# Hybrid mLSTM/HGRN2 layer on one core: value turns split between VectorE and ScalarE, exponential-first gates, a sixth side bank

## The chip, the cores and the metric

The kernel runs on one core of a Trainium2 chip. A core has a matrix engine (TensorE, PE in the profile, with its weight loads as PEld), VectorE (DVE), ScalarE (ACT), GpSimd (POOL) and SyncE (SP), which issues DMAs. Each engine works through its own instruction list in order, and the engines wait for one another by semaphores. SBUF and PSUM have 128 partitions; the kernel uses PSUM as eight banks.

The metric is the device time of one execution in microseconds. Before the change it is 2304.08 us, the median of 3 runs (2303.45 to 2305.43).

## The reference

One layer of a decoder on 320 tokens (256 of a prompt, 8 x 8 of a sample) with D_MODEL 2048, all in float32. Two token mixers, an mLSTM (4 heads, key 256, value 512) and an HGRN2 (8 heads, key 128, value 256), read one input projection. They are recurrences that carry a state over the tokens and that the reference evaluates in chunks of 64. Cut to what matters here:

```python
proj = jnp.einsum('btd,de->bte', x, w_in)
(ml_q, ml_k, ml_v, ml_i, ml_f, ml_o, hg_q, hg_f, hg_i, hg_g, gate_a, gate_b) = jnp.split(proj, offs, axis=-1)
...
h, C, n, m = _mlstm(q, k, v, ig, lf, C0, n0, m0)
branch_a = layernorm(h) * ml_norm_g * jax.nn.sigmoid(ml_o)
f = lbh + (1.0 - lbh) * jax.nn.sigmoid(_heads(hg_f, HG_HEADS))
o, S = _hgrn2(hq, jnp.log(f), 1.0 - f, _heads(hg_i, HG_HEADS), S0)
branch_b = o * rsqrt(mean(o * o) + eps) * hg_norm_g * jax.nn.silu(hg_g)
ya = branch_a @ w_branch_a
yb = branch_b @ w_branch_b
merged = jax.nn.sigmoid(gate_a) * ya + jax.nn.sigmoid(gate_b) * yb
x1 = LayerNorm(ALPHA * x + merged @ w_out)
y = LayerNorm(ALPHA * x1 + jnp.square(jax.nn.relu(x1 @ w_up)) @ w_down)
# out: y, and the new states C, n, m, S
```

## The kernel before

**Main work.** All activations lie channel by token: 128 channels on the partitions, 320 tokens in the columns. The weights are cut into 304 tiles of 128 output channels by 2048 input channels. Each tile is summed into one PSUM bank by 48 matmuls of 128x320, 16 input blocks by 3 products: weights and activations are each split into a high and a low fp32r part (`wh`/`wl`, `xh`/`xl`), and the products are high-high, high-low and low-high. A tile comes in two units of 128x1024 weights. For each unit SP loads `wr`, ACT makes `wh` from it (a copy, in line 350, the helper that records every ACT operation), and DVE makes `wl = wr - wh` (line 497). Three such `wh`/`wl` buffers go round; ACT may write one when PE has finished the unit that used it.

**Order.** The main matmuls have a fixed order: 4 mLSTM heads (tiles mv, mk, mq), with gate tiles ga between them, 8 HGRN heads (two gate tiles, then hf, hq and two hi each), 16 output-gate tiles o, the rest of the gates, then hg, wa, wb, wo, and the two feed-forward products. All else is written as chains (Python generators) which a planner, `Sched`, puts between the main matmuls while the program is built. The planner keeps a clock per engine and prices each operation by functions: `act(n)` is (112 + n)/1.2 ns, `dve(n)` (66 + n)/0.96, `dve_t(n)` for DVE transposes. A side matmul is placed in PE's list when the planner's clock says that its operand is ready, with 450 ns to spare (`PE_LAT`). Nothing is reordered at run time: if an operand comes later than planned, PE waits with all that stands behind.

**Banks.** Three PSUM banks (`mbank`) take the main tiles and five (`sbank`) the side matmuls, from the start until tile hg 0 and on until wo 0, where they are dealt out anew.

**Values.** The values of a head come from the main tiles as channel by token and are needed as token by channel. `turn` does this by DVE transposes, which turn blocks of 32x32, in 24 pieces a head: each piece reads one group of 32 partitions and writes another. For an mLSTM head (`m_V`) they are 16 of 32x256 and 8 of 32x128, for an HGRN head (`h_i`) 16 of 32x128 and 8 of 32x64. In `h_i` the last pieces are followed by a high part on ACT (`rh<-f`, 64x256), a low part on DVE (line 1488 before, 1492 after), and two side matmuls `rh,ra` of 128x256, which spread the sample's values over the partitions (lines 1492 and 1493 of before, with `self.spread`).

**Gates.** `sigmoid` takes a gate's main bank. DVE writes min(-p, 87) to SBUF (line 1309), ACT takes the exponential, ACT the logarithm of 1 plus it, scaled, ACT the exponential of minus that, which gives the reciprocal, and DVE does a correction step in two operations (lines 1315 and 1316). 72 tiles pass through it. `free` names the bank that is released as soon as the first operation has read it.

**Outputs.** `h_out` normalises an HGRN head's prompt output (`rms`, with a copy, a Square and one-column operations) and transposes two blocks of 128x256 (line 1631). `ev_o` multiplies an output gate with the mLSTM output and splits the product into high and low parts (line 1672) for the products wa.

Of the kernel before, what the change touches and what calls it, by code (L numbers as in the profile page):

```python
# [12 lines left out]
AF = mybir.ActivationFunctionType  # L13
ALU = mybir.AluOpType
# [6 lines left out]
TOK = 320  # L21
KT = 16
MH, DK, DV = 4, 256, 512
HH, HK, HV = 8, 128, 256
EPS = 1e-5
LN_SH = 62
# [218 lines left out]
def wait(*evs):  # L245
    return ("wait", evs)


def acq(pool, n=1):
    return ("acq", pool, n)  # L250


def rel(pool, item):
    return ("rel", pool, item)


def post(ev):
    return ("set", ev)


def act(n, psum=False, ptr=0):
    return ((61 if psum else 112) + n) / 1.2 + 93 * ptr


def dve(n, psum=False, mode=1, ptr=0):
    return ((62 if psum else 66) + n / mode) / 0.96 + 55 * ptr


def dve_t(n):
    return 155.0 + 1.07 * n  # L270


def pe_f(n, m=128):
# [40 lines left out]
class Program:  # L314
# [48 lines left out]
    def carve(self):  # L363
# [12 lines left out]
        self.Part = Part  # L376
        A, B, C, R = Part(self.f1), Part(self.f2), Part(self.f3), Part(self.ra[:, 0:6400])

# [5 lines left out]
        self.vr = Pool([A.three(4, 320)])  # L384
        self.kw = Pool([B.three(2, 320)])
        self.bc = Pool([B(712) for _ in range(2)])
        self.eb0 = B(512)
        self.eb = Pool([self.eb0])
        self.stg = Pool([B(256) for _ in range(2)])
        self.qn0 = B(256)  # L390
        self.qn = Pool([self.qn0])
# [190 lines left out]
    def before(self, i, t):  # L582
        s = self.s
        kind, h, c = t[:3]
        if kind == "mv" and c == 0:
            s.until(lambda: self.vr.free and self.qk.free)
            self.m_start(h)
            self.vr.free.sort(key=lambda x: x[0])
            self.mh[h]["vr"] = self.vr.free.pop(0)[1]
        elif kind == "hf":  # L590
            s.until(lambda: self.hs.free)
            if h == 0:
                s.spawn(self.m_after(), 0)
            self.h_start(h)
        elif kind == "o" and h == 0:
            s.until(lambda: all(m["end"].t is not None for m in self.mh))
        elif kind == "hg" and h == 0:
            s.until(lambda: all(m["end"].t is not None for m in self.hh))
            self.carve_m()
            self.carve_b()  # L600
            B = self.Part(self.f2)
            for pool in (self.sg, self.sg, self.sr, self.ld, self.ld, self.ld):
                pool.free.append((s.t["pe"], B(320)))
        if kind in ("o", "wa", "hg", "wb"):
            s.spawn(self.fetch(kind, h), 1)
        elif kind == "mk" and h == 0 and c == 0:
            self.load_ev.t = s.t["pe"]
            self.dma(self.lmask, self.d["lmask"])
        elif kind == "wo" and h == 0:
            s.until(lambda: len(self.sbank.free) >= 5)  # L610
            self.mbank.free += self.sbank.free[:3]
            del self.sbank.free[:3]
            self.hl_free += [(s.t["pe"], x) for x in self.wx[:4]]
            R = self.Part(self.wxv[4].rearrange("p x s v -> p (x s v)"))
            self.lns = [R.three(2, TOK) for _ in range(3)]
            s.spawn(self.ln_x(), 1)
        elif kind == "dn" and c == 3 and h == 0:
            self.carve_x()
        elif kind == "dn" and c == 0 and h == 0:
            s.spawn(self.xs_(), 0)  # L620
        elif i == len(TILES) - 8:
            for j in range(MH):
                s.spawn(self.m_C(j), 3)
            for j in range(HH):
                s.spawn(self.h_S(j), 3)
# [519 lines left out]
    def turn(self, to, x):  # L1145

        v = self.nc.vector
        n = x.shape[1]
        for a in range(4):
            p = slice(32 * a, 32 * a + 32)  # L1150
            col = lambda y: y.rearrange("p (c a k) -> p a c k", a=4, k=32)[:, a]
            for b in range(4):
                q = slice(32 * b, 32 * b + 32)
                i = x[p, :, 0:NP_].rearrange("p c (i b k) -> p b i c k", b=4, k=32)[:, b]
                o = to[q, 0:2, :].rearrange("p i (c a k) -> p a i c k", a=4, k=32)[:, a]
                yield ("dve", dve_t(64 * n), lambda: v.transpose(o, i))  # L1156
            for b in range(2):
                o, i = col(to[64 + 32 * b:96 + 32 * b, 2, :]), x[p, :, NP_ + 32 * b:NP_ + 32 * b + 32]
                yield ("dve", dve_t(32 * n), lambda: v.transpose(o, i))  # L1159

    def later(self):
        e = Ev()
# [140 lines left out]
    def sigmoid(self, p, out, r, free=()):  # L1303

        v = self.nc.vector
        yield ("dve", dve(TOK, True), lambda: v.tensor_scalar(out, p, -1.0, 87.0, ALU.mult, ALU.min))  # L1309
        for pool, x in free:  # L1310
            yield rel(pool, x)
        yield ("act", act(TOK), lambda: self.A(out, out, AF.Exp))
        yield ("act", act(TOK), lambda: self.A(r, out, AF.Ln, scale=2.0 ** -LN_SH, bias=self.ln_b))
        yield ("act", act(TOK), lambda: self.A(r, r, AF.Exp, scale=-1.0, bias=self.exp_b))
        yield ("dve", dve(TOK), lambda: v.scalar_tensor_tensor(out, out, 1.0, r, ALU.add, ALU.mult))  # L1315
        yield ("dve", dve(TOK), lambda: v.scalar_tensor_tensor(out, out, 2.0, r, ALU.subtract, ALU.mult))  # L1316

    def ev_hf(self, h, c, b):
# [296 lines left out]
    def h_out(self, h):  # L1615
        nc, v, m = self.nc, self.nc.vector, self.hh[h]
        if h:
            yield wait(self.hh[h - 1]["o"])
        yield wait(m["aT"], m["I"])
        at, it = m["at"], m["it"]  # L1620
        on = yield acq(self.on)
        yield post(m["o"])
        b = yield acq(self.sbank)
        yield ("pe", pe_f(256), lambda: self.mm(b[:, 0:256], at[:, 0:128], it[:, 0, :], start=True, stop=True))
        yield ("pe", pe_f(256), lambda: self.mm(b[:, 256:512], at[:, 368:496], it[:, 0, :], start=True, stop=False))
        yield ("pe", pe_f(256), lambda: self.mm(b[:, 256:512], at[:, 128:256], it[:, 1, :], start=False, stop=True))
        for i in range(2):
            yield from self.rms(b[:, 256 * i:256 * i + 256], on[:, i, :], 128)
        yield rel(self.sbank, b)
        for i in range(2):  # L1630
            yield ("dve", dve_t(256), lambda: v.transpose(on[:, i, :], on[:, i, :]))  # L1631
        yield from self.place(self.rows_to(self.oH[h]), on[:, 0:2, :].rearrange("p i v -> p (i v)").rearrange("p (b c) -> p b c", c=32))
        done = self.later()
        yield wait(m["S"])
        ob = m["ob2"]
        yield from self.rms(ob[:, 0:256], on[:, 2, :], 128)
        yield rel(self.sbank, ob)
        yield rel(self.at, at)
        b = yield acq(self.sbank)
        for j in range(2):  # L1640
            yield ("pe", PE_T, lambda: nc.tensor.transpose(b[:, 128 * j:128 * j + 128], on[:, 2, 128 * j:128 * j + 128], self.ident))
        o = yield acq(self.ho)
        for j in range(2):
            yield ("act", act(64, True), lambda: self.A(by_row(o, 64 * j, False), by_row(b, 128 * j, True)))
        yield rel(self.sbank, b)
        yield ("sp", 620, lambda: self.dma(
            self.oL[h].rearrange("(j p) t -> p j t", p=128), o[:, 0:128].rearrange("p (j t) -> p j t", t=64)))
        for j in range(2):
            yield post(self.oT_ev[2 * h + j])
        yield wait(self.later())  # L1650
        yield rel(self.ho, o)
        yield wait(done)
        yield rel(self.on, on)
        yield wait(m["SP"], m["sdone"])
        yield rel(self.it, it)
        yield rel(self.hs, m["set"])
        yield post(m["end"])
# [33 lines left out]
    def ev_o(self, j, c, b):  # L1691
        v = self.nc.vector
        g = yield acq(self.sg)
        r = yield acq(self.sr)
        yield from self.sigmoid(b[:, :TOK], g, r, ((self.mbank, b),))
        yield rel(self.sr, r)
        x = yield from self.fetched("o", j)
        yield ("dve", dve(TOK, ptr=1), lambda: v.scalar_tensor_tensor(g, g, self.vec[:, V_MLG + j:V_MLG + j + 1], x, ALU.mult, ALU.mult))  # L1698
        yield rel(self.ld, x)
        yield from self.split(g, self.bah[:, j, :], self.bal[:, j, :])  # L1700
        yield rel(self.sg, g)
        yield post(self.ba_ev[j])
# [386 lines left out]
```

## Time and profile before

| what | value |
| --- | --- |
| median of 3 runs | 2304.08 us |
| profiled execution, whole | 2302.73 us |
| its span in the profile | 2300.8 us |
| PE busy | 2289.6 us, 15592 matmuls |
| DVE busy | 1458.9 us, 2634 instructions |
| ACT busy | 1036.6 us, 1653 instructions |
| POOL busy | 13.5 us |
| PE's granted clock | full speed in all 40 slices |
| DMA | 424.94 MB, a mean of 185 GB/s |

The profile is of one execution; PE, PEld, DVE, ACT and POOL are engines, and `L350` is line 350 of the kernel. A row of the groups reads: line, engine, operation, out <- in with partitions x elements, count, busy us and mean ns of one, and then the idle time of the engine just before these instructions and what ended it. Names of tiles are those of the memory that they lie in: `f`, `f3h` are float32 scratch, `ra`, `rh` fp32r scratch, `misc` single columns, `bank` a PSUM bank. The matmuls are pipelined, so a matmul's own length (0.31 us) is longer than the time from one to the next (0.146 us). A row of waits reads: engine and what waited, what it waited for, total us, times, longest us.

### The profile page before, as it was taken

The numbers are of one execution on the slowest core, as the hardware profiler recorded it, in microseconds if no ns is written. First come the engines' busy times: TensorE is split into PE (matmuls) and PEld (weight loads), VectorE is DVE, ScalarE is ACT, GpSimd is POOL, SyncE is SP. The second block draws the span as 40 slices with busy tenths as digits, with TensorE's granted clock in tenths as the row PEclk, the third lists the DMA queues.
The fourth block names the chain that finished last, engine by engine and source line by source line (L and its number), as shares of the span: only waits on it lengthen the run. The fifth ranks groups of instructions, "written<-read, shape, count | busy, mean of one in ns | idle before, by whom it ended". The sixth has DMA issues, their size and how long they took to land.

```text
span 2300.8 us, 38921 instructions
## 1 busy us (share of the span) xinstructions
PE 2289.6 (100%) x15592; PEld 2246.1 (98%) x15592; DVE 1458.9 (63%) x2634; ACT 1036.6 (45%) x1653; POOL 13.5 (1%) x37
## 2 busy tenths in 40 slices
PE   9999999999999999999999999999999999999998
PEld 9999899999999999999999999999999999999998
DVE  6786786788888886555555767654444444444455
ACT  5443445455555565444433446533433343234334
POOL 0000000000000000000000000000000000000000
PEclk9999999999999999999999999999999999999999
DMA  7667977755565564555545644444444444444475
GB/s 284 211 186 259 295 250 229 259 176 185 191 207 187 166 198 167 180 174 170 176 172 175 214 163 147 147 147 149 154 147 150 152 147 153 149 147 154 149 228 193
DMA packets 214574, 424.94 MB, mean 185 GB/s; under 512 B 83572, under 2 KB 110068, under 8 KB 213368
## 3 DMA queue, kind: packets, MB, share of 16 engines
q1 hardware_dynamic: 209512, 415.97, 53.7%
q0 software_dynamic: 4736, 6.29, 1.0%
q8 instruction: 122, 2.00, 0.3%
q14 instruction: 60, 0.49, 0.1%
q10 hardware_dynamic: 144, 0.20, 0.0%
HBM read 371.48 MB, written 50.90 MB: 184 GB/s over the span
## 4 chain that ended last, share of the span: by engine, by line
PE 69%; DVE 3%; ACT 1%; issue 0%; ACTq 0%; DVEq 0%
PE bank L356 69%; DVE wl L497 1%; ACT wh L350 0%; DVE f L1156 0%; DVE f L1445 0%; ACT f L350 0%; DVE f3m L1973 0%; DVE f3m L1980 0%; ACT f3m L350 0%; DVE f L1159 0%; DVE f L1315 0%; DVE f L1316 0%; DVE f L1631 0%; DVE f L1698 0%; DVE f L1309 0%
## 5 line engine op out<-in xcount | busy, mean ns | idle before, releaser
L356 PE MATMUL bank<-xh,wh 128*128 128x320 f32 (+1 forms) x2504 | 794.6, 318 | 0.0
L356 PE MATMUL bank<-xh,wl 128*128 128x320 f32 (+1 forms) x2504 | 774.8, 310 | 0.0
L356 PE MATMUL bank<-xl,wh 128*128 128x320 f32 (+1 forms) x2504 | 772.2, 309 | 0.0
L497 DVE TENSOR_TENSOR wl<-wr,wh 128x1024 fp32r<-128x1024 f32 x440 | 538.7, 1224 | 361.4 <-ACT wh L350 358.3
L350 ACT ACTIVATE wh<-wr 128x1024 fp32r<-128x1024 f32 x440 | 465.4, 1058 | 524.7 <-PE bank L356 495.6
L356 PEld LDWEIGHTS bank<-xh,wh 128*128 128x128 f32 x2504 | 472.0, 189 | 17.2 <-issue 15.3
L356 PEld LDWEIGHTS bank<-xl,wh 128*128 128x128 f32 x2504 | 471.5, 188 | 3.3
L356 PEld LDWEIGHTS bank<-xh,wl 128*128 128x128 f32 x2504 | 471.8, 189 | 0.2 <-DVE wl L497 0.2
L497 DVE TENSOR_TENSOR bb<-wr,bb 128x1024 fp32r<-128x1024 f32 x162 | 198.5, 1225 | 193.7 <-ACT bb L350 193.5
L350 ACT ACTIVATE bb<-wr 128x1024 fp32r<-128x1024 f32 x162 | 171.6, 1059 | 294.6 <-PE bank L356 277.5
L356 PE MATMUL bank<-ra,wh 128*128 128x320 f32 x1008 | 275.9, 309 | 0.7 <-DVE ra L1672 0.7
L356 PE MATMUL bank<-ra,bb 128*128 128x320 f32 x1096 | 255.2, 309 | 0.0
L356 PE MATMUL bank<-xh,bb 128*128 128x320 f32 (+1 forms) x1136 | 253.8, 309 | 0.0
L356 PE MATMUL bank<-rxb,bb 128*128 128x320 f32 x1088 | 249.0, 309 | 0.0
L356 PEld LDWEIGHTS bank<-xh,bb 128*128 128x128 f32 x1136 | 191.0, 188 | 0.0
L356 PE MATMUL bank<-rxb,wh 128*128 128x320 f32 x608 | 187.5, 308 | 0.0
L356 PE MATMUL bank<-rxb,wl 128*128 128x320 f32 x608 | 187.5, 308 | 0.0
L356 PEld LDWEIGHTS bank<-ra,bb 128*128 128x128 f32 x1096 | 184.9, 187 | 0.0
L356 PEld LDWEIGHTS bank<-rxb,bb 128*128 128x128 f32 x1088 | 184.2, 187 | 0.0
L356 PEld LDWEIGHTS bank<-ra,wh 128*128 128x128 f32 x1008 | 180.9, 187 | 0.9 <-DVE ra L1672 0.9
L356 PE MATMUL bank<-xl,bb 128*128 128x320 f32 (+1 forms) x568 | 175.5, 309 | 0.0
L356 PE MATMUL bank<-bb,wh 128*128 128x320 f32 (+1 forms) x536 | 119.0, 313 | 0.0
(259 smaller groups left out, 2244.4 us busy)
## 6 DMA issues: line engine op xcount, KB each, us to landing
wr<-wt SPq DMA_DIRECT2D x602, 512.0 KB, 3.3
rx<-C SPq DMA_DIRECT2D x34, 256.0 KB, 5.6
Cs<-rx SPq DMA_DIRECT2D x34, 256.0 KB, 4.8
f<-C SPq DMA_DIRECT2D x30, 256.0 KB, 5.5
Cs<-f SPq DMA_DIRECT2D x30, 256.0 KB, 4.1
f<-first SPq DMA_DIRECT2D x6, 704.0 KB, 9.6
vD<-ra SPq DMA_DIRECT2D x4, 1024.0 KB, 5.2
f<-S SPq DMA_DIRECT2D x8, 512.0 KB, 5.0
```

Of the source, the lines that this page charges most:

```text
L350: return self.nc.scalar.activation(out, in_, func, **kw)
L356: self.nc.tensor.matmul(*a, **kw)
L497: self.V().tensor_tensor(lo, raw, hi.bitcast(F32), ALU.subtract)
```

## The change

Six edits are made together.

1. `turn`: one DVE transpose turns the whole value tile in place (128x1280 in an mLSTM head, 128x640 in an HGRN head). The 24 pieces become ACT copies of the same shapes, from one group of 32 partitions to another; each waits for the transpose.
2. `sigmoid`: ACT takes exp(-p) from the bank at once, and the bank is released after it. DVE then clamps the result to 1e38 and adds 1, ACT takes the scaled logarithm and the exponential, and DVE's correction is a plain product and one more operation.
3. A sixth side bank: from the first mk tile until hg 0, one main bank is lent to the side matmuls, so that the main tiles have two.
4. `h_out`: one transpose of 128x512 in place of two of 128x256.
5. `ev_o`: from the eighth output gate on, the split waits for an event of the last HGRN head (`aT`, or `sdone` from the thirteenth).
6. The planner's price `dve_t` of a DVE transpose.

```diff
@@ dve_t
-    return 155.0 + 1.07 * n
+    return 295.0 + 1.05 * n
@@ before()
             self.carve_b()
+            self.mbank.free.append(self.sbank.free.pop())
...
         elif kind == "mk" and h == 0 and c == 0:
+            s.until(lambda: self.mbank.free)
+            self.sbank.free.append(self.mbank.free.pop())
@@ turn()
         n = x.shape[1]
+        t = yield ("dve", dve_t(TOK * n), lambda: v.transpose(x, x))
         for a in range(4):
...
-                yield ("dve", dve_t(64 * n), lambda: v.transpose(o, i))
+                yield ("act", act(64 * n), lambda: self.A(o, i), (t,))
...
-                yield ("dve", dve_t(32 * n), lambda: v.transpose(o, i))
+                yield ("act", act(32 * n), lambda: self.A(o, i), (t,))
@@ sigmoid()
-        yield ("dve", dve(TOK, True), lambda: v.tensor_scalar(out, p, -1.0, 87.0, ALU.mult, ALU.min))
+        yield ("act", act(TOK, True), lambda: self.A(out, p, AF.Exp, scale=-1.0))
         for pool, x in free:
             yield rel(pool, x)
-        yield ("act", act(TOK), lambda: self.A(out, out, AF.Exp))
-        yield ("act", act(TOK), lambda: self.A(r, out, AF.Ln, scale=2.0 ** -LN_SH, bias=self.ln_b))
-        yield ("act", act(TOK), lambda: self.A(r, r, AF.Exp, scale=-1.0, bias=self.exp_b))
-        yield ("dve", dve(TOK), lambda: v.scalar_tensor_tensor(out, out, 1.0, r, ALU.add, ALU.mult))
+        yield ("dve", dve(TOK, mode=2), lambda: v.tensor_scalar(out, out, 1e38, 1.0, ALU.min, ALU.add))
+        yield ("act", act(TOK), lambda: self.A(r, out, AF.Ln, scale=2.0 ** -LN_SH))
+        yield ("act", act(TOK, False, 1), lambda: self.A(r, r, AF.Exp, scale=-1.0, bias=self.exp_b))
+        yield ("dve", dve(TOK), lambda: v.tensor_tensor(out, out, r, ALU.mult))
         yield ("dve", dve(TOK), lambda: v.scalar_tensor_tensor(out, out, 2.0, r, ALU.subtract, ALU.mult))
@@ h_out()
-        for i in range(2):
-            yield ("dve", dve_t(256), lambda: v.transpose(on[:, i, :], on[:, i, :]))
+        yield ("dve", dve_t(512), lambda: v.transpose(on[:, 0:2, :], on[:, 0:2, :]))
@@ ev_o()
+        if j > 6:
+            yield wait(self.hh[HH - 1]["aT" if j < 12 else "sdone"])
         yield from self.split(g, self.bah[:, j, :], self.bal[:, j, :])
```

Since the planner sets the order from its prices, the change also moves instructions. Three places in the values of the fifth HGRN head show it. In the rows a shape like 32x4x32 is a piece of 128 columns in four strips, and 32x2x32 one of 64.

On ACT, before, the high part `rh` of these values (third row) stands among copies for other work:

```order
L350 ACTIVATE wh<-wr 128x1024
L350 ACTIVATE ra<-bank_86 32x256
L350 ACTIVATE rh<-f_76 64x256
L350 ACTIVATE ra<-bank_86 32x256
L350 ACTIVATE f_76<-bank_85,misc 128x256
```

On ACT, after, the pieces stand ahead of it, between the rms of the head before, a gate's Exp (from `bank_82`) and Ln, and the weights `wh`; these are the last rows of the burst:

```order
L350 ACTIVATE f_76<-bank_82 128x320
L350 ACTIVATE f_76,misc<-bank_81 128x256
L350 ACTIVATE wh<-wr 128x1024
L350 ACTIVATE f_76<-f_75 32x4x32 x2
L350 ACTIVATE f_76<-f_75 32x2x32 x2
L350 ACTIVATE f_76<-f_75 32x4x32 x4
L350 ACTIVATE f_76<-f_75 32x2x32 x2
L350 ACTIVATE f_76<-f_76 128x320
L350 ACTIVATE misc<-misc 128x1
L350 ACTIVATE rh<-f_76 64x256
L350 ACTIVATE wh<-wr 128x1024
```

The 24 pieces have come into ACT's list, with one `wh` right ahead of them and another among them.

On DVE, before, the last piece (line 1159) and, seven rows behind it, the low part of the same values (line 1488):

```order
L987 TENSOR_TENSOR f_76<-f_75,f_76 128x16x8
L497 TENSOR_TENSOR wl<-wr,wh 128x1024
L1059 TENSOR_TENSOR misc<-misc 128x1
L1416 TENSOR_TENSOR f_75<-f_75 128x16x8
L1159 STREAM_TRANSPOSE f_76<-f_75 32x2x32
L1471 COPY_PREDICATED f_75<-lmask,bank_88 128x16x8
L1060 TENSOR_TENSOR misc<-misc 128x1
L1418 TENSOR_TENSOR f_75<-f_75 128x16x8
L1061 TENSOR_SCALAR misc<-misc 128x1
L1062 TENSOR_TENSOR misc<-misc 128x1
L1419 TENSOR_TENSOR f_75<-f_75 128x16
L1488 TENSOR_TENSOR rh<-f_76,rh 64x256
```

On DVE, after, from the last but one weight part to the low part (line 1492):

```order
L1384 TENSOR_TENSOR ra<-f_75,ra 128x800
L497 TENSOR_TENSOR wl<-wr,wh 128x1024
L1316 TENSOR_SCALAR f_76<-f_76 128x320
L1667 TENSOR_SCALAR misc<-misc 128x1
L1059 TENSOR_SCALAR misc<-misc 128x1
L497 TENSOR_TENSOR wl<-wr,wh 128x1024
L1319 TENSOR_TENSOR f_76<-f_76 128x320
L1062 TENSOR_TENSOR misc<-misc 128x1
L1492 TENSOR_TENSOR rh<-f_76,rh 64x256
```

The pieces are gone from DVE's list, and a `wl`, which waits for the `wh` behind ACT's `rh`, stands three rows ahead of the low part.

On PE, before, the first spread matmul of these values follows 147 main matmuls later in the program than it does after the change:

```order
L356 MATMUL bank_82<-xh,wl 128x320
L1641 MATMUL bank_84<-cst,f_76 128x128
L356 MATMUL bank_88<-rh,ra 128x256
L356 MATMUL bank_82<-xh,wh 128x320
L356 MATMUL bank_82<-xl,wh 128x320
```

On PE, after, it stands three main matmuls into the tile hf of the next head:

```order
L356 MATMUL bank_86<-f_75 128x32
L356 MATMUL bank_82<-xh,wh 128x320
L356 MATMUL bank_82<-xl,wh 128x320
L356 MATMUL bank_82<-xh,wl 128x320
L356 MATMUL bank_84<-rh,ra 128x256
```

The spread has moved up, from the last tile of the next head to its first.

## The prediction

> **What bounds the kernel now.** I read the page's totals first, then PE's waits, then its busy share in stretches, then the groups of the lines that change.
>
> ```profile
> span 2300.8 us, 38921 instructions
> PE 2289.6 (100%) x15592; PEld 2246.1 (98%) x15592; DVE 1458.9 (63%) x2634; ACT 1036.6 (45%) x1653; POOL 13.5 (1%) x37
> PE bank L1530 <- DVE f L987: 1.5, 3, 0.7
> PE bank L356 <- DVE rh L1488: 1.1, 2, 0.6
> PE bank L356 <- POOL ones L640: 1.0, 1, 1.0
> PE bank L1212 <- DVE f L1049: 0.7, 1, 0.7
> PE bank L356 <- DVE ra L1672: 0.7, 1, 0.7
> PE bank L356 <- DMA rx<-C: 0.2, 1, 0.2
> ```
>
> PE is busy all the time. The six rows below the totals are all that it waits for: 5.2 us together (columns: total, times, longest). No edit can win more than that while PE's instructions stay the same, and the change neither adds nor drops one on PE. Four of the six rows (1.5 + 1.1 + 0.7 + 0.2 = 3.5 us) are waits for DVE or a DMA inside the heads, where DVE is relieved; POOL's is the start, L1672's the output gates.
>
> ```profile
> 500.00:600.00 100.00, 99.95 (x703) 97.28 (x702) 86.16 (x240) 56.01 (x123) 0.73 (x2) 1.00 0.62 197
> 700.00:800.00 100.00, 98.78 (x701) 95.22 (x700) 83.82 (x230) 57.19 (x129) 0.37 (x1) 1.00 0.56 180
> 1000.00:1100.00 100.00, 100.00 (x683) 100.00 (x682) 58.54 (x80) 44.01 (x57) 0.00 (x0) 1.00 0.51 171
> ```
>
> These are stretches of 100 us (busy time and count of PE, PEld, DVE, ACT, POOL, then PE's clock). At 1000 us there are only main matmuls: 100.00/683 = 0.1464 us each, and a tile of 48 lasts 7.03 us. At 500 to 800 us, among the HGRN heads, DVE is 84 to 86% busy and ACT 56%. So the change takes work from the fuller engine. But PE runs in order: what decides is whether a side matmul's operand is there when PE gets to it.
>
> **The turn.** The rows of the 288 small transposes, of two wide ones, and of the ACT copies nearest to the new pieces:
>
> ```profile
> L1156 DVE STREAM_TRANSPOSE f<-f 32x128 f32<-32x128 f32 x96 | 29.0, 303 | 2.3
> L1156 DVE STREAM_TRANSPOSE f<-f 32x256 f32<-32x256 f32 x64 | 27.9, 436 | 1.5
> L1159 DVE STREAM_TRANSPOSE f<-f 32x64 f32<-32x64 f32 x48 | 11.4, 238 | 1.0
> L1159 DVE STREAM_TRANSPOSE f<-f 32x128 f32<-32x128 f32 x32 | 9.7, 304 | 0.8
> L1156 DVE STREAM_TRANSPOSE f<-f3h 32x128 f32<-32x128 f32 x32 | 9.7, 302 | 0.7
> L1159 DVE STREAM_TRANSPOSE f<-f3h 32x64 f32<-32x64 f32 x16 | 3.8, 238 | 0.4
> L1631 DVE STREAM_TRANSPOSE f<-f 128x256 f32<-128x256 f32 x16 | 7.0, 435 | 0.0
> L1090 DVE STREAM_TRANSPOSE f<-f 128x512 f32<-128x512 f32 x8 | 5.7, 709 | 0.2
> L350 ACT ACTIVATE rh<-f 64x256 fp32r<-64x256 f32 x8 | 3.3, 415 | 2.1 <-DVE f L1159 1.9
> L350 ACT ACTIVATE ra<-f 64x128 fp32r<-64x128 f32 x4 | 1.2, 308 | 0.1
> L350 ACT ACTIVATE f<-f 64x64 f32<-64x64 f32 x4 | 1.0, 253 | 0.9 <-DVE f L907 0.8
> ```
>
> DVE loses the first six rows, 91.5 us. It gains four transposes of 128x1280 and eight of 128x640. The two wide rows give (709 - 435)/256 = 1.07 ns a column, so 0.85 us for 640 and 1.53 us for 1280: 12.9 us in all. The two 256-wide transposes of the head's output become one of 512: 2 x 0.435 - 0.709 = 0.16 us less for each of 8 heads. DVE nets about -80 us.
>
> ACT gains the 288 copies. By the last three rows a copy of 256, 128 and 64 columns takes 0.415, 0.308 and 0.253 us. Whether two of them overlap is shown by these stretches (start, length, xcount):
>
> ```profile
> 605.69 0.76 ACT L350 ACTIVATE ra<-bank 32x256 fp32r<-32x256 f32 x2 [1.60 <-PE bank L1530]
> 610.49 0.34 ACT L350 ACTIVATE f<-bank 128x64 f32<-128x64 f32 x2
> 614.70 0.77 ACT L350 ACTIVATE f<-bank 32x32 f32<-32x32 f32 x4
> L350 ACT ACTIVATE ra<-bank 32x256 fp32r<-32x256 f32 x32 | 12.0, 374 | 5.5 <-PE bank L1530 5.1
> L350 ACT ACTIVATE f<-bank 128x64 f32<-128x64 f32 x32 | 5.5, 215 | 2.0 <-PE bank L1641 1.0 <-PE bank L1212 0.9
> L350 ACT ACTIVATE f<-bank 32x32 f32<-32x32 f32 x32 | 6.0, 186 | 1.8 <-PE bank L356 1.4
> ```
>
> Two copies over all 128 partitions take 0.34 us, not 2 x 0.215 = 0.43: about 0.09 overlaps. Copies on 32 partitions don't: two of 0.374 take 0.76 and four of 0.186 take 0.77, some 0.01 apart. Every new piece is on 32 partitions, so I take 0.32 us (128) and 0.265 (64): an HGRN head's burst is 16 x 0.32 + 8 x 0.265 = 7.2 us. An mLSTM head's is 16 x 0.427 + 8 x 0.32 = 9.4 us. With overlap by 0.095 it would be 16 x 0.213 + 8 x 0.158 = 4.7 us; these are the two ends. The planner's own price, (112 + n)/1.2, is 0.20 and 0.147, a burst of 4.4 us. So ACT falls some 2.8 us behind the plan in each HGRN head. Before, the planner charged 0.292 and 0.223 for the pieces on DVE, which took 0.303 and 0.238: that plan was nearly right.
>
> The Trainium skill (ScalarE: Activation LUTs, What ACT_TABLE_LOAD costs) gives an ACTIVATE with immediates 186 ns + 0.833 ns per element and lets back-to-back ones overlap by about 93 ns. That would be 0.2 and 0.146 us a piece. The pair on 128 partitions agrees; the 32-partition runs don't, and the measurement decides for these pieces.
>
> **What the lateness hits.** These rows carry the chain:
>
> ```profile
> L350 ACT ACTIVATE wh<-wr 128x1024 fp32r<-128x1024 f32 x440 | 465.4, 1058 | 524.7 <-PE bank L356 495.6 <-issue 21.2 <-DMA wr<-wt 7.1
> L497 DVE TENSOR_TENSOR wl<-wr,wh 128x1024 fp32r<-128x1024 f32 x440 | 538.7, 1224 | 361.4 <-ACT wh L350 358.3 <-PE bank L356 1.2
> L1488 DVE TENSOR_TENSOR rh<-f,rh 64x256 fp32r<-64x256 f32 x8 | 3.4, 421 | 0.8 <-ACT rh L350 0.7
> 612.13 0.36 PE L356 MATMUL bank<-rh,ra 128*128 128x256 f32 x1 [0.63 <-DVE rh L1488]
> L350 ACT ACTIVATE f<-bank 128x320 f32<-128x320 f32 x57 | 24.7, 437 | 95.3 <-PE bank L356 95.2
> L350 ACT ACTIVATE f<-f 128x320 f32<-128x320 f32 x138 | 63.0, 457 | 17.4 <-DVE f L1309 14.8 <-DVE f L1852 2.4
> L350 ACT ACTIVATE f<-bank,misc 128x256 f32<-128x256 f32 x24 | 11.3, 470 | 22.6 <-DVE misc L1062 22.5
> L350 ACT ACTIVATE f<-f,misc 128x320 f32<-128x320 f32 x162 | 91.1, 563 | 32.4 <-DVE f L1937 21.3 <-DVE f L1323 7.0
> ```
>
> After the burst come ACT `rh<-f` 64x256, DVE `rh` (L1488 before, L1492 after), and PE's first `rh,ra` matmul, for which PE already waited 0.63 us at 612. Worked for the fifth head, from the moment when PE finishes the weight unit whose buffer ACT needs. On ACT: `wh` 1.06, the burst 7.2, the rms copy 0.47, a gate's Exp 0.44, a Square of the rms copy's size, 0.47 at most, a second `wh` 1.06, the gate's Ln 0.46, a one-column op (at most a 64-column copy's 0.25), `rh` 0.42; less some 0.1 for each overlap of 128-partition neighbours: 11.3 to 11.6. DVE has a `wl` ahead of L1492, which waits for the next `wh` (12.6) and ends at 13.8; then L1319 and L1062, about 0.5 by L1488's 0.42 for 256 columns, and L1492 0.42: ready at 14.7. PE meets its matmul after 76 main matmuls and seven side ones, counted as a main one each: 83 x 0.1464 = 12.15. The stall is 2.5 us. The same sum for the other heads, with their own orders, gives 0.2 for the first (its place is further off) and 2.0, 2.1, 2.2, 2.3, 2.3, 2.4: together 16.0 us. In the mLSTM heads the pieces' readers and the next weights lie one to three us beyond the burst's end: 0 to 0.3 each, counted as 0.
>
> **The other edits.** They are priced from the last four rows above and from these:
>
> ```profile
> L1309 DVE TENSOR_SCALAR f<-bank 128x320 f32<-128x320 f32 x70 | 34.2, 488 | 40.3 <-PE bank L356 39.7
> L1315 DVE SCALAR_TENSOR_TENSOR f<-f 128x320 f32<-128x320 f32 x70 | 34.3, 490 | 13.5 <-ACT f L350 13.0
> L1316 DVE SCALAR_TENSOR_TENSOR f<-f 128x320 f32<-128x320 f32 x70 | 34.3, 490 | 1.5
> L1323 DVE TENSOR_SCALAR f<-f,misc 128x320 f32<-128x320 f32 x6 | 2.6, 435 | 0.1
> ```
>
> A gate keeps three ops on each engine. ACT: 0.457 + 2 x 0.563 becomes 0.437 + 0.457 + 0.563, 0.126 less; 72 gates, -9 us. DVE: the clamp moves from PSUM (0.488) to SBUF, 0.435 at most by L1323, half of that if immediates run faster: -4 to -18 us. All of it lies beside PE. The main bank is now freed by ACT, perhaps behind part of a burst. Moving one bank leaves main two: a bank is wanted again one tile, 7.03 us, after its last matmul. In the fifth head the Exp follows 14 pieces and runs some 3 us after its tile's end, leaving about 4 us. Cost 0; if that cover went, the next tile would start late by the rest. The sixth side bank removes no row of PE's waits: those name data. The two new waits of an output gate stand on events whose matmuls PE has passed by then: 0; behind them waits only that gate's own split.
>
> **Sum.** 2302.73 us is the profiled execution (span 2300.8 and 1.93 outside it). -3.5 for DVE's waits (0 to -3.5), +16.0 for eight stalls (0 to 20): 2315.2. The median of the runs lies 1.35 above that execution: 2316.6; I say 2316.
>
> **Rivals.** 0.2% is 4.6 us, about what a measurement of this kernel can tell from no change: 2299.5 to 2308.7.
> - The pieces overlap like the 128-partition ops. For it: the pair of 0.34. Against: both 32-partition rows. Each burst is then 2.5 us shorter, all stalls but a few tenths go, and only the 3.5 remain: 2304.08 - 3.5 = 2300.6, not slower. At a mean of about 0.23 us a piece (a 5.5 us burst) stalls of 8 x 0.6 and the gain cancel; below that the change wins. The Trainium skill's rule quoted above (ScalarE: Activation LUTs) leads to this time.
> - Stalls come, but at a third to a half of the size: the `wh` whose buffer I took as late may start sooner, or PE's side matmuls cost more than I counted. 16 becomes 5 to 8: 2304.08 - 3.5 + 5 to 8, 2305.6 to 2308.6, no change.
> - A second wait follows in each head: ACT, 2.8 us late, delivers `wh` late for the next main unit, or a gate's bank is freed late, for 1 us or more beyond the first stall: +8 to +12 more, 2324 to 2328. Against it: ACT is idle 44% of these stretches and three weight buffers stand ahead.
>
> **Chances.** Forecast (2308.7 to 2322) 0.65; a third to a half 0.16; overlap 0.10; second waits 0.09. Overlap ends faster by over 0.2% only if it also clears nearly all 5.2 us: 0.04, with 0.02 for gains that I don't see. So faster 0.06, same 0.20, slower 0.74. The range runs from 2302 (most of the overlap case below it) to 2323.
>
> **What would show it.** Right: the `f<-f` 32x128 copies on ACT at 0.30 to 0.33 us and back to back without overlap; PE's waits headed by DVE `rh` L1492, about eight times 2 us; DVE some 90 us less busy, ACT 85 more. Wrong: 24 pieces within 5 us, no wait for L1492, or waits of the main matmuls for `wh` or for a bank at the top of the list.

## The result, and the profile after

The changed kernel takes 2332.59 us (median of 4 runs, 2329.23 to 2334.51) against 2304.67 us before on the same chip: a ratio of 1.012, 95% interval 1.0103 to 1.0138. It is slower by 28 us; the forecast was slower by 12. Its profiled execution took 2331.51 us, with a span of 2329.4 us.

The totals of the page of the changed kernel, and then all that PE waited for:

```profile
span 2329.4 us, 38935 instructions
PE 2298.8 (99%) x15592; PEld 2255.8 (97%) x15592; DVE 1351.8 (58%) x2350; ACT 1110.0 (48%) x1941; POOL 13.6 (1%) x37
```
```profile
PE bank L356 <- DVE rh L1492: 18.6, 8, 2.6
PE bank L356 <- DVE rx L1275: 2.9, 3, 1.6
PE bank L356 <- DVE ra L967: 1.2, 1, 1.2
PE bank L356 <- POOL ones L643: 1.0, 1, 1.0
PE bank L356 <- DVE ra L1675: 0.7, 1, 0.7
PE bank L356 <- DVE f L1201: 0.3, 1, 0.3
PE bank L1534 <- DVE f L990: 0.2, 1, 0.2
```

DVE is relieved by 107 us and ACT carries 73 more (the forecast had 90 and 85), and the time got worse: neither engine was the bound. The new head of the list is the wait that the forecast named, for the low part of the HGRN values at L1492, eight times, 18.6 us. Below it are 4.4 us of waits in the mLSTM heads (L1275, L967, L1201), which are new. The low part is the operation that was L1488 before, where it cost 1.1 us. Of the other waits of before, those for L1049 and for the DMA are gone, and for L987 (now L990) 0.2 us are left.

One stall in full, that of the fifth head, the one worked out in the prediction. The timelines of ACT, DVE and PE in the changed kernel (start, length, operation):

```profile
644.49 1.05 ACT L350 ACTIVATE wh<-wr 128x1024 fp32r<-128x1024 f32 x1
645.56 3.45 ACT L350 ACTIVATE f<-f 32x128 f32<-32x128 f32 x11
649.13 0.41 ACT L350 ACTIVATE rh<-f 64x256 fp32r<-64x256 f32 x1
649.57 1.06 ACT L350 ACTIVATE wh<-wr 128x1024 fp32r<-128x1024 f32 x1
```
```profile
650.65 1.23 DVE L497 TENSOR_TENSOR wl<-wr,wh 128x1024 fp32r<-128x1024 f32 x1 [3.37 <-ACT wh L350]
651.80 0.49 DVE L1319 TENSOR_TENSOR f<-f 128x320 f32<-128x320 f32 x1
652.20 0.15 DVE L1062 TENSOR_TENSOR misc<-misc 128x1 f32<-128x1 f32 x1
652.38 0.42 DVE L1492 TENSOR_TENSOR rh<-f,rh 64x256 fp32r<-64x256 f32 x1
```
```profile
650.18 0.31 PE L356 MATMUL bank<-xh,wl 128*128 128x320 f32 x1
652.95 0.55 PE L356 MATMUL bank<-rh,ra 128*128 128x256 f32 x1 [2.46 <-DVE rh L1492]
653.30 0.47 PE L356 MATMUL bank<-xh,wh 128*128 128x320 f32 x1
653.57 0.47 PE L356 MATMUL bank<-xl,wh 128*128 128x320 f32 x1
```

The second ACT row merges the last ten pieces and the Ln that stands among them: eleven operations in 3.45 us, a mean of 0.31 us, with no overlap. `rh` ends at 649.54, but DVE has a `wl` first, which waits for the `wh` of 649.57; so L1492 starts at 652.38. PE stands from 650.5 to 652.95. The last two PE rows show the part that was not forecast: the next main matmuls start 0.27 us apart instead of 0.147. PE's clock has fallen. The stretches around this stall, and then around that of the seventh head (columns: stretch, length, PE busy, matmuls, granted clock, share and rate of the DMA):

```profile
648.83:652.24 3.41, 1.66 (x12) 1.00 0.22 85
652.24:655.65 3.41, 2.70 (x10) 0.50 0.71 225
655.65:659.07 3.42, 3.42 (x14) 0.50 0.95 253
659.07:662.48 3.41, 3.41 (x24) 1.00 0.74 228
```
```profile
761.47:764.88 3.41, 1.70 (x12) 1.00 0.52 187
764.88:768.29 3.41, 3.41 (x26) 1.00 1.02 357
```

The granted clock is one half for 6.83 us, and in the second half of that PE, though busy all the time, does 14 matmuls where it would do some 23. That costs about as much as the stall itself: some 2.7 us, by the distances of 0.27 and 0.147 us from the stall's end on. But not every stall has one: the seventh head's is 2.52 us long and the clock stays full. In the whole trace, up to the last matmul, the clock is one half in five places, here for 6.83 us and in the others for 3.41: behind four of the eight stalls (the fourth, fifth, sixth and eighth head) and behind one in the mLSTM heads.

The 28.6 us of span add up like this: PE's listed waits 24.9 - 5.2 = 19.7 us; the time between starts of neighbouring matmuls of 128x320 or 128x322 over the full array, summed over the trace, 2128.0 us against 2119.1, and with five pairs fewer: 9.6 us of lower clock. Together 29.3.

The groups whose durations the forecast had to estimate:

```profile
L350 ACT ACTIVATE f<-bank 128x320 f32<-128x320 f32 x127 | 55.1, 435 | 171.6 <-PE bank L356 171.2
L350 ACT ACTIVATE f<-f 32x128 f32<-32x128 f32 x128 | 39.3, 307 | 4.1 <-DVE f L1152 2.3
L350 ACT ACTIVATE f<-f 32x256 f32<-32x256 f32 x64 | 26.5, 415 | 2.2 <-DVE misc L1062 1.0 <-DVE f L1152 0.5
L350 ACT ACTIVATE f<-f 32x64 f32<-32x64 f32 x48 | 12.2, 253 | 0.6
L1152 DVE STREAM_TRANSPOSE f<-f 128x1280 f32<-128x1280 f32 x4 | 6.0, 1494 | 0.0
L1152 DVE STREAM_TRANSPOSE f<-f 128x640 f32<-128x640 f32 x6 | 5.0, 836 | 0.0
L1316 DVE TENSOR_SCALAR f<-f 128x320 f32<-128x320 f32 x70 | 22.5, 321 | 0.0
```

### The profile page after: what moved, and what is told of

It reads as the page before. It is cut to its first block, busy times and chain, and to the rows that moved or that the text cites. A ratio compares the mean times of both kernels' runs of the same rounds, so it can differ in the third digit from the quotient of the medians.

```text
span 2329.4 us, 38935 instructions
## 1 busy us (share of the span) xinstructions
PE 2298.8 (99%) x15592; PEld 2255.8 (97%) x15592; DVE 1351.8 (58%) x2350; ACT 1110.0 (48%) x1941; POOL 13.6 (1%) x37
## 4 chain that ended last, share of the span: by engine, by line
PE 90%; ACT 6%; DVE 3%; DMA 1%; issue 1%; SPq 0%; ACTq 0%; POOL 0%; DVEq 0%; POOLq 0%
PE bank L356 89%; ACT f L350 4%; ACT wh L350 1%; DVE wl L497 1%; DMA rx<-C 0%; DMA wr<-wt 0%; DMA Cs<-rx 0%; DVE f L1152 0%; DVE f3m L1978 0%; DVE f3m L1985 0%; DVE rx L1275 0%; DVE rh L1492 0%; ACT f3m L350 0%; DVE f L1319 0%; DVE ra L967 0%
## 5 line engine op out<-in xcount | busy, mean ns | idle before, releaser
L350 ACT ACTIVATE f<-f 32x128 f32<-32x128 f32 (+7 forms) x413 | 153.4, 372 | 90.3 <-DVE f L1316 72.7
```

The source lines that it names most:

```text
L350: return self.nc.scalar.activation(out, in_, func, **kw)
```

## The experiments

The theory after the result: the pieces on 32 partitions take 0.12 us more than the planner's price, so PE's list calls for operands before they are there; the longer of the stalls also lower PE's clock for some microseconds. Rivals: the copies are too much for ACT wherever they stand (rival 1); or gates, banks or another edit cost the time, not the turn (rival 2). All times below are medians beside runs of the kernel before on the same chip (2303.7 to 2304.0 us).

**The price alone.** In the changed kernel:

```diff
-                yield ("act", act(64 * n), lambda: self.A(o, i), (t,))
+                yield ("act", act(64 * n) + 118.0, lambda: self.A(o, i), (t,))
...
-                yield ("act", act(32 * n), lambda: self.A(o, i), (t,))
+                yield ("act", act(32 * n) + 118.0, lambda: self.A(o, i), (t,))
```

> The changed kernel, the planner's price of each ACT piece raised by 118 ns (to what the pieces took there: 0.307 us and 0.012 to the next, against 0.200 planned). Theory (pieces on 32 partitions don't overlap, the plan is 2.8 us too early in each HGRN head, PE stalls, and its clock falls after the longer stalls): PE's wait for the low part at L1492 falls from 18.6 to under 3 us, the granted clock rises from 0.995 to 0.999, time 2300 to 2306 us. Rival 1 (the copies are too much work for ACT wherever they stand: they push the weights back): waits go over to others, above 8 us in all beyond the 5.2 of the kernel before, 2315 us or more. Rival 2 (gates or banks cost the time, not the turn): 2325 us or more.

Measured: 2297.29 us, ratio 0.9976 (0.9964 to 0.9988). Every instruction of the change is still there; only the plan differs, and 35 us are gone. The profile page's totals and all of PE's waits in this kernel:

```profile
PE 2286.5 (100%) x15592; PEld 2245.1 (98%) x15592; DVE 1348.5 (59%) x2350; ACT 1110.8 (48%) x1941; POOL 13.4 (1%) x37
```
```profile
PE bank L1030 <- DVE f L990: 1.1, 1, 1.1
PE bank L356 <- POOL ones L643: 1.0, 1, 1.0
PE bank L356 <- DVE ra L1675: 0.7, 1, 0.7
PE bank L1644 <- ACT f L350: 0.2, 1, 0.2
```

ACT is as busy as in the changed kernel (1110.8 against 1110.0 us), and nothing waits for L1492, nor for L1275 or L967 in the mLSTM heads. Rival 1 falls: the work fits. The time is 2.7 us below the expected range, and the run is faster than the kernel before.

**The turn back on DVE,** the rest of the change kept:

```diff
-        t = yield ("dve", dve_t(TOK * n), lambda: v.transpose(x, x))
...
-                yield ("act", act(64 * n), lambda: self.A(o, i), (t,))
+                yield ("dve", 155.0 + 1.07 * 64 * n, lambda: v.transpose(o, i))
...
-                yield ("act", act(32 * n), lambda: self.A(o, i), (t,))
+                yield ("dve", 155.0 + 1.07 * 32 * n, lambda: v.transpose(o, i))
```

> The changed kernel with the 24 small transposes of a head back on DVE, at their old price; gates, banks, the output's transpose and the order of the output gates stay changed. Theory: no wait for L1492 over 2 us in all, clock 0.999, 2299 to 2305 us. Rival 2 (gates or banks cost the time): 2315 us or more. Rival 1 says the same as the theory here.

Measured: 2297.12 us, ratio 0.9971 (0.9959 to 0.9984), clock 0.999, with no wait for the low part; 1.9 us below the expected range. Rival 2 falls: gates, banks, output and guards cost nothing. With the turn on the fuller engine the kernel is as fast as with the turn on ACT at a right price.

**The turn alone,** on the kernel before, with the edit of `turn` from the diff and nothing else:

> The kernel before with the turn alone changed (one wide DVE transpose, 24 ACT copies), at the planner's prices of the change. Theory: the stalls at the low part come with the turn alone, 10 to 19 us of waits for it and 4 to 10 us of lower clock: 2318 to 2335 us. Rival 2: under 2310 us.

Measured: 2324.17 us, ratio 1.0092 (1.0077 to 1.0107). The time is as expected, the place only in part. The head of PE's waits in this kernel:

```profile
PE bank L356 <- ACT f L350: 9.3, 9, 2.0
PE bank L356 <- DVE rh L1489: 3.1, 4, 2.0
PE bank L356 <- ACT f3h L350: 2.8, 2, 1.6
```

The low part (here L1489) has 3.1 us, not 10 to 19; most waits stand at other matmuls that read what ACT wrote. The clock is one half in two stretches of 3.41 us, some 3 us of loss by the distances above (0.27 against 0.147 us), less than the 4 to 10 expected. Where the lateness of ACT is paid depends on what the plan has put next behind it.

**The same, priced right** (118 ns more a piece, as above):

> The kernel before with the turn alone changed, as in the run that took 2324.2 us, but its ACT pieces priced 118 ns higher, at what they take. If the loss is the price and not the move: no stall of 2 us, clock 0.999, 2297 to 2305 us. If the copies are too much for ACT beside the old gates: 2312 us or more.

Measured: 2298.4 us, ratio 0.9976 (0.9966 to 0.9985), clock 1.0. The one constant in the price is worth 26 us here too.

**Half of the correction,** 59 ns a piece in the changed kernel:

> The changed kernel with half of the correction, 59 ns a piece: each HGRN burst is then 1.4 us longer than planned. If PE's stall is what the plan is short of: eight stalls of 0.7 to 1.4 us, 6 to 10 us in all, too short to lower the clock (0.999): 2303 to 2310 us. If the planner's margin of 0.45 us and other slack cover it: 2296 to 2300 us.

Measured: 2312.3 us, ratio 1.0038 (1.0025 to 1.0051), clock 0.999. PE's waits begin with

```profile
PE bank L356 <- DVE rh L1492: 8.8, 8, 1.7
PE bank L356 <- DMA rx<-C: 2.2, 1, 2.2
```

Half of the error gives half of the stalls (8.8 us against 18.6), as the first case said; a DMA's 2.2 us in an mLSTM head, which was not expected, with 3.41 us of half clock behind it, puts the time 2 us above the range. From no correction to half to full: 2332.6, 2312.3, 2297.3 us.

**Only the one place moved.** In the changed kernel the planner takes the low part for ready 3 us later, and all prices stay:

```diff
-        yield ("dve", dve(256), lambda: v.tensor_tensor(lo, it[64:128, 2, :], hi.bitcast(F32), ALU.subtract))
+        t = yield ("dve", dve(256), lambda: v.tensor_tensor(lo, it[64:128, 2, :], hi.bitcast(F32), ALU.subtract))
         yield post(m["I"])
+        late = Ev()
+        late.t = t + 3000.0
+        yield wait(late)
```

> The changed kernel with its prices as they are, only that the planner takes the values' low part of each HGRN head (L1492, here L1496) for ready 3.0 us later before it places the two spread matmuls in PE's list. Theory (the loss of the HGRN heads sits at this one place, because PE's list calls the operand too early): waits for the low part under 3 us, clock 0.998 or 0.999, 2302 to 2310 us (the 4 us of waits in the mLSTM heads stay). Rival 1 (ACT stays 2.8 us behind its plan, so the next reader of ACT's work stalls instead): other waits of 10 us or more, 2316 us or more.

Measured: 2328.64 us, ratio 1.0103 (1.0086 to 1.012), clock 0.995. My theory of the one place fell, and what rival 1 foretold for this run came: other waits of 19 us, 4.7 of them in the mLSTM heads. The head of PE's list:

```profile
PE bank L356 <- DVE f L1422: 7.8, 6, 1.7
PE bank L356 <- DVE rx L1275: 4.7, 3, 1.9
PE bank L1537 <- DVE f L990: 3.6, 4, 1.9
PE bank L356 <- DVE f3h L1422: 3.3, 2, 1.7
```

No wait for the low part is left, but L1422, a product of the HGRN scan, is late instead. DVE's timeline of this kernel shows by what:

```profile
654.47 1.23 DVE L497 TENSOR_TENSOR wl<-wr,wh 128x1024 fp32r<-128x1024 f32 x1 [3.03 <-ACT wh L350]
...
657.28 1.22 DVE L497 TENSOR_TENSOR wl<-wr,wh 128x1024 fp32r<-128x1024 f32 x1
658.42 0.32 DVE L1316 TENSOR_SCALAR f<-f 128x320 f32<-128x320 f32 x1
658.65 0.15 DVE L1063 TENSOR_TENSOR misc<-misc 128x1 f32<-128x1 f32 x1
658.72 0.32 DVE L1422 TENSOR_TENSOR f<-f 128x160 f32<-128x160 f32 x1
```

DVE stands 3.03 us at a `wl` because ACT's `wh` is late behind the burst, and everything in DVE's list shifts with it, whether it has to do with the values or not. The error sits in the planner's clock for ACT, not at one operand. Both runs together (this one and the price) leave rival 1 only this much: ACT is behind the plan, but not overloaded.

**Idle work in place of the stall.** In the changed kernel, ahead of the first spread matmul of each HGRN head, 16 matmuls on data that lie there, whose result is overwritten:

```diff
+    def spread_mm(self, b, bv, g, vst):
+        for _ in range(16 if g == 0 else 0):
+            self.mm(b[:, 0:TOK], self.xh[:, 0, 0:128], self.xh[:, 0, :], start=True, stop=True)
+        self.mm(bv[:, g, :], self.spread[:, g, :], vst[:, 0, :], start=True, stop=True)
```

> The changed kernel with 16 idle matmuls of 128x320 (0.147 us each, 2.35 us; on data that lie there, their result is overwritten) ahead of the first spread matmul of each HGRN head: work in place of the stall, 128 matmuls more. Theory that the clock falls because PE stands still for 2 us and more: waits for L1492 under 4 us, clock 0.998 or 0.999, and the kernel is faster than the changed one by 5 to 9 us, 2323 to 2328 us (the stalls of the mLSTM heads and their clock stay). Rival (the clock loss has another cause, such as the load or the time): the clock stays 0.995 and the time 2332 to 2336 us.

> As the run with 16 idle matmuls, but 8 (1.18 us) ahead of the first spread of each HGRN head, so that stalls of 0.5 to 1.6 us stay there (some 9 us in all). If only a stall of about 2 us or more lowers the clock: clock 0.998 or 0.999 and the time of the run with 16, 2323 to 2326.5 us. If the clock is lost in proportion to the time that PE stands still: clock 0.997, 2327 to 2330 us.

Measured: 2324.71 us with 16 (2323.35 to 2325.37; ratio 1.0089, 1.0074 to 1.0104) and 2325.79 us with 8 (2324.53 to 2327.16; 1.0095, 1.0079 to 1.011), both at a clock of 0.999. The wait for the low part in the one and the other:

```profile
PE bank L356 <- DVE rh L1492: 0.4, 2, 0.2
```
```profile
PE bank L356 <- DVE rh L1492: 9.2, 8, 1.4
```

128 matmuls of pure waste make the changed kernel 7.9 us faster, since PE no longer stands still long enough there to lose its clock (one stretch of half clock is left, in an mLSTM head). With 8 of them PE still stands 9.2 us, in stalls of at most 1.4, and keeps its clock throughout: the loss is not in proportion to standing still.

How long is too long? In the traces of all 14 kernels the granted clock falls 16 times before the last matmul, 15 times for 3.41 us and once for twice that, and its changes lie whole multiples of 3.41 us apart. So I cut each trace into stretches of 3.41 us at these bounds and took PE's idle time in each stretch at full clock:

| PE idle in the stretch | stretches | followed by half clock |
| --- | --- | --- |
| 1.75 us or more | 9 | 9 |
| 1.18 to 1.74 us | 26 | 7 |
| less | all others | 0 |

So what counts is how a stall falls on these bounds, and not only how long it is. The fifth head's 2.46 us leave 1.75 idle in one stretch, and the clock falls; the seventh head's 2.52 are cut into 0.81 and 1.71, and it does not. What decides between 1.18 and 1.74 us was not found.

**What each other edit is worth,** from the version with the right price: without the sixth side bank, and with the gates of before.

> The changed kernel with the pieces at their measured price, without the sixth side bank. If the bank brings nothing of the gain over the kernel before: 2295.5 to 2299.5 us. If it carries the gain (PE's short waits for a side bank): 2301 to 2305 us.

> The changed kernel with the pieces at their measured price and the gates as before (DVE's clamp first). If the gates bring nothing of the gain: 2295.5 to 2299.5 us. If they carry it: 2301 to 2305 us. The theory (what counts is whether PE's list agrees with the operands' times, and the gates were priced right before and after) says the first.

Measured: 2295.49 us without the bank (ratio 0.9963, 0.9948 to 0.9978), 2299.65 us with the old gates (0.9982, 0.9973 to 0.9991). The bank brings nothing. With the old gates the time is 2.4 us above that with the new ones, just outside the first range. All of PE's waits in the version with five banks:

```profile
PE bank L356 <- POOL ones L640: 1.0, 1, 1.0
PE bank L356 <- DVE ra L1672: 0.7, 1, 0.7
```

It is the fastest of all, 8 us under the kernel before: only the start and the output gates' 0.7 us are left.

**The gates alone,** on the kernel before with the `sigmoid` of the diff:

> The kernel before with the gates alone changed (ACT's exponential first). The run with the old gates in an else unchanged kernel lost some 2 us: if the gates bring that by themselves, 2299 to 2303 us; if they bring nothing without the rest, 2303 to 2305 us.

Measured: 2302.57 us, ratio 0.9992 (0.9983 to 1.0002): not told from no change. Without the waits of edit 5, 15 of the 16 low parts of the output gates, which are written to `ra`, start here before the last head's last `rh,ra` matmul (in the kernel before, 5 do), and this version's results are wrong, though its instructions are the same in number and kind. That these writes destroy what the head still reads is likely, since the waits of edit 5 keep them apart, but it was not tested. By the letter 2302.57 us lies in the first range; but with a new wait of 2.3 us for ACT in it, and 3.41 us of half clock behind that, it says little of what the gates are worth.

**The old price of DVE's transposes** in the version with five banks:

> The version with five side banks and the measured piece price (2295.5 us), with the planner's old price of DVE transposes, 155 + 1.07 n, which by the traces is right within 31 ns for 256 to 1280 columns, where the new one is 80 to 140 ns too high. If a right price brings something: 2293 to 2295 us; if the small surplus is harmless: 2295 to 2297 us.

Measured: 2299.46 us (2297.77 to 2301.3), ratio 0.9978 (0.9968 to 0.9987): 4 us slower than with the new price, against both cases. (By the rows above the new price is some 125 to 150 ns too high, where the expectation has 80 to 140: it is 967 ns for 640 columns that took 836, and 1639 for 1280 that took 1494.) PE's waits that came with it:

```profile
PE bank L356 <- ACT f L350: 1.3, 2, 1.1
PE bank L1213 <- DVE f L1049: 1.1, 1, 1.1
```

The second row's DVE operation is no transpose, and the first row's is ACT's. So among plans that are right, each re-planning moves 2 to 4 us about, and a difference of that size between two versions is not the worth of an edit.

## Why the prediction was half right

**Right: the mechanism, its place and its sign.** The pieces measured 0.307 and 0.253 us against the 0.308 and 0.253 taken from 64-partition rows, without overlap (the rival of overlap is out). The stall of the fifth head was put at 2.5 us and is 2.46. The sum of the eight was put at 16.0 and is 18.6; the difference lies mostly in the first head, put at 0.2, where PE waits 2.34 us at 442 us. I had taken that head's place for further off than it is.

**Wrong: the clock.** The sum had no term for PE's clock; that step was priced at nothing without being named. It cost 9.6 us, and the run with idle matmuls shows that it hangs on the stalls. The trace of before could hardly tell: its longest stall is 1.0 us, and its clock 1.00 in the stretches shown. What the runs showed in its place: half clock behind four of the eight stalls and one other. The Trainium skill (TensorE: Matmul & The Clock Gate, HAM oscillation — how this bites in real kernels) warns in that section of PE gaps over about 3.4 us. By that rule stalls of 2.5 us would have cost no clock; here four waits of 2.29 to 2.56 us did, and so did one of 1.18 in the run with 16 idle matmuls, and the measurement decides. The same page of the Trainium skill (What's actually happening) lets the gate look at windows that run freely, so that where a gap falls in them matters; the traces, with changes of the clock whole multiples of 3.41 us apart, agree with that.

**Wrong: the mLSTM heads at 0.** "0 to 0.3 each, counted as 0" became 4.4 us. I looked at the readers of the turned values, and the lateness was paid by others: L1275 frees, one by one, the four side banks that the next update takes together, and at the longest of its waits it stands on DVE behind a `wl` that had waited 2.84 us for ACT. That they come from the price is shown, since they vanish with it.

**Half right: the gain.** -3.5 us came as -1.1 - 1.3 - 0.7 - 0.2 = -3.3. But that "no edit can win more" than the 5.2 us of listed waits was wrong: the priced version's span is 5.3 us shorter and the one with five banks 6.6, while their waits fell by 2.2 and 3.5 us. PE's "busy" time fell with them, by 3.1 and 2.7 us at the same number of matmuls. In the priced version the distances between neighbouring main matmuls sum to 2118.6 us against 2119.1 before, so nearly all of the 3.1 lies beside side matmuls, in time that no list of waits shows. Busy time is no floor.

2316 + 9.6 + 4.4 + 2.6 is 2332.6, the measured time. That it fits to a tenth is luck: the terms are of one execution of 2331.51 us, and there waits and clock sum to 0.7 us more than its span grew. The rival "a second wait follows in each head", put at 0.09 and 2324 to 2328, was nearest in size, but not in kind: what followed four of the eight stalls was a slow clock.

**The other edits** were rightly costed at nothing on the path. The gate's bank, the sixth side bank and the waits of the output gates show in no list of the changed kernel. DVE's new clamp is 0.321 us, inside the bounds.

## What to carry to other kernels

When work moves to another engine in a kernel whose order is planned beforehand, look first at the price the plan gives it there: 0.12 us too little on each of the 24 copies of a head cost 35 us, while the engine had half its time free. Operations over few partitions are to be priced from rows with few partitions. Give a stall of a busy PE of some 2 us a term for the clock (here 9.6 us behind 19.7 us of added waits), or keep PE going with idle matmuls.

## What the runs showed of the hardware

ACT copies on 32 partitions follow each other with no overlap, at 0.31 us for 128 columns, where two on 128 partitions overlap by some 0.09 us; the pieces cross from one group of 32 partitions to another at no extra cost (of the 128 pieces of 128 columns in the changed kernel most cross and some do not, and all took 0.29 to 0.313 us). PE's granted clock falls to one half, with main matmuls 0.27 us apart instead of 0.147, for 3.41 us (once for 6.83): always behind a stretch of 3.41 us between its bounds in which PE was idle for 1.75 us or more, at times from 1.18 us on, and never below that in these traces.
